# Five conditioning chunks of layer 1 accumulated during attention instead of during the output projection

## The chip, the core and the metric

The kernel runs on one core of a Trainium2 chip. The metric is the device time of one execution in microseconds; the time shown is the median of three runs. One more execution was recorded by the hardware profiler, and all rows below come from it.

Engines: TensorE (PE; its weight loads are listed as PEld), VectorE (DVE), ScalarE (ACT), GpSimd (POOL), and SyncE (SP), which only issues DMAs. Every engine works through its own queue in order.

## The reference

Two layers over 512 latent tokens of width 2048, with 256 context tokens. Layer 0 is attention: eight heads with low-rank queries and keys (A, the "long" heads here) and eight grouped-query heads (B, the "short" heads), a SiLU gate and one output projection. Layer 1 mixes by a Fourier transform. Each layer is modulated by a vector computed from `c`:

```
def modulation(cvec, ada_w, ada_b):
    m = jax.nn.silu(cvec) @ ada_w + ada_b        # 2048 -> 6144
    return jnp.split(m, 3, axis=-1)              # shift, scale, gate

def gated_out(y_a, y_b, gate, w_out):
    y = jnp.concatenate([y_a..., y_b...], axis=-1)
    return (y * jax.nn.silu(gate)) @ w_out       # the output projection, 2048 x 2048

x = post_norm(x, o_lat, g_l, ln_g[i], ln_b[i])
```

The 6144 columns of one layer's modulation are handled in twelve chunks of 512. Layer 1 needs its shift and scale (chunks 0 to 7) when its transforms begin, right behind the output projection of layer 0.

## The kernel before

All matmul operands are split in two (`split`, L41 and L44): ScalarE casts the high part, VectorE subtracts to get the low part, and `mm3` (L54) does three matmuls high x high, high x low, low x high.

**A conditioning chunk** is accumulated on VectorE, not on TensorE. `ada_steps` takes the weights of a chunk in pieces of `nk` k's: `ada_load` (L62 by way of `load`) fetches a piece of 128 x `nk` x 512 on SP, and for each k one instruction multiplies it by the column of `silu(c)` and adds it to `acc` (L195 the first, L197 the others), 16 in all. `tick` advances this generator by one piece; it is called from inside other loops, which is how the work is spread. When a chunk is complete, the next tick runs `ada_col`: four small matmuls with `ones` (L219, eight passes in the trace) turn the 512 sums into four columns in a PSUM tile, and VectorE adds the bias (L223). The loads are always pinned: `keep_in_program_order` puts an instruction behind the one traced before it on the same engine. Other instructions may be moved by the planner that orders each engine's queue when the program is built. Chunks of layer 1: 4, 0 and 5 are done before attention (in `lateral`, behind the four gate chunks of layer 0), 1, 6, 2, 7 and 3 during the output projection, 8 to 11 in the gates of layer 1.

**Attention** (`attention`) begins by splitting the six query tiles `self.cq` into `cqh` and `cql`; from then on `cq0` to `cq5` are dead, as are `sqa` and `rq`, all in the pool `keep`. Its main loop runs 64 turns, one for each head and block of 128 queries; turns 0 to 31 are the long heads, 32 to 63 the short ones. A turn does, in this order on TensorE: `fills` (projections for coming heads: `q_nope`, `q_pe` with rotary work on VectorE at L685 and L688, `k_nope`, `v_a`), `turn(i)` (six transposes of the probabilities into two PSUM tiles `pt` of the pool `psT`, which has two banks; ScalarE and VectorE empty them into `pth` and `ptl`, L778 and L779), `late` fills, `values(i - 2)` and `scores(i + 2)`, followed by the softmax on VectorE, ScalarE and GpSimd (L752 to L761). From turn 27 on the scores come ahead of `turn`. `self.pinned` is true throughout, so TensorE's order is the traced one. Two banks of `acc` serve all projections and value products.

**The output projection** (`out_proj`, called from `mixer_out`) makes four blocks of 512 columns (n). In each, 16 k's of weights are loaded two at a time, split, and multiplied with four token tiles into four PSUM banks `oacc` (there are eight); in the last block the tokens come in two groups. A block closes with the gate (`tg`, L972), the residual (L976) and statistics (L977) on VectorE. `mac_start` stands in `mixer_out` with `nk` = 2; `tick` is called after each k, from k 8 of block 0 to the end of block 2, and `mac_rest` in block 3. `ada_col` takes an `oacc` bank for its product.

Of the kernel before, what the change touches and what calls it, by code (L numbers as in the profile page):

```python
# [10 lines left out]
F32 = mybir.dt.float32  # L11
# [13 lines left out]
class Build:  # L25
# [666 lines left out]
    def attention(self, keep):  # L692
        nc, d = self.nc, self.d
        self.y_d = [self.dr.tile([128, 512], F32, name=f"y{h}") for h in range(16)]
        with ExitStack() as s:
# [17 lines left out]
            cq = []  # L713
# [152 lines left out]
            def q_b(h):  # L866
# [7 lines left out]
                def score(ps, qt):  # L874
                    o = 128 * qt
                    for a, b in segs:
                        self.mm3(ps[:, a:b], cut(qb, o, o + 128), cut(kb, a, b), True, True)
                heads[8 + h] = {"score": score, "col": 4 + 4 * h,
                                "v": lambda t: [v[:, t, 128 * j:128 * j + 128] for v in vb]}

            fills, late = {0: [(v_a, 0, 2)]}, {}
            for hp in range(4):
                b, n = 8 * hp, hp + 1
# [25 lines left out]
            scores(0)  # L909
            v_a(0, 1)  # L910
            scores(1)
            for i in range(64):
                for f, *a in fills.get(i, []):
                    f(*a)
                if 26 < i < 62:
                    scores(i + 2)
                turn(i)
                for odd in (0, 1):
                    if i in late and i % 2 == odd:
                        f, *a = late[i]  # L920
                        f(*a)
                    if i >= 2 and odd == 0:
                        values(i - 2, i % 2)
                if i < 27:
                    scores(i + 2)
            for i in (62, 63):
                values(i, i % 2)
            self.pinned = False

    def out_proj(self, w, nk, y, gate_d, res, xp, rawp, pg, tp, acp, st, kq, hold, done, every, late, first=lambda n: None):  # L930
        nc = self.nc
        for n in range(4):
            first(n)
            gt = tp.tile([128, 512], F32, name="gate", bufs=1)
            self.load(gt, gate_d[n])
            acs = [acp.tile([128, 512], F32, name="oacc") for _ in range(4)]
            groups = [(0, 1, 2, 3)] if n < 3 else [(0, 1), (2, 3)]
            for group in groups:
                end = group[-1] == 3 and n == 3
                held = []  # L940
                for q in range(nk // kq):
                    for kk in range(kq):
                        y(kq * q + kk)
                    raw = rawp.tile([128, kq, 512], F32, name="raw")
                    self.load(raw, w(n, q))
                    for kk in range(kq):
                        k = kq * q + kk
                        yh, yl = y(k)
                        hi = pg.tile([128, 512], F32R, name="pgh")
                        lo = pg.tile([128, 512], F32R, name="pgl")  # L950
                        self.split(raw[:, kk, :], hi, lo)
                        if end and k >= nk - hold:
                            held.append((k, hi, lo))
                            continue
                        for t in group:
                            o = 128 * t
                            self.mm3(acs[t], (yh[:, o:o + 128], yl[:, o:o + 128]), (hi, lo), k == 0, k == nk - 1)
                        if every and n < 3 and (n or k >= 8):
                            self.mac_hold = n == 0
                            self.tick()  # L960
                if n == 3 and not end:
                    self.mac_rest()
                if end:
                    late()
                for t in group:
                    o = 128 * t
                    for k, hi, lo in held:
                        self.mm3(acs[t], (y(k)[0][:, o:o + 128], y(k)[1][:, o:o + 128]), (hi, lo), False, k == nk - 1)
                    xr = tp.tile([128, 512], F32, name="xr")
                    self.load(xr, res(t, n))  # L970
                    g = tp.tile([128, 512], F32, name="tg")
                    ins = nc.vector.tensor_mul(out=g, in0=acs[t], in1=gt)  # L972
                    if end and t == 3:
                        self.tc.keep_in_program_order(ins)
                    xs = xp[t][:, 512 * n:512 * n + 512]
                    nc.vector.scalar_tensor_tensor(out=xs, in0=xr, scalar=ALPHA, in1=g, op0=ALU.mult, op1=ALU.add)  # L976
                    nc.vector.bn_stats(out=st[t][:, n, :], in_=xs)  # L977
                    if n == 3:
                        done(t)

    def mixer_out(self, s):
# [7 lines left out]
        with ExitStack() as c:  # L989
# [19 lines left out]
            def first(n):  # L1009
                if n == 1:  # L1010
# [4 lines left out]
                    for t, nme in zip(gb, ("lng", "lnb")):  # L1015
                        self.load(t, d[nme][0].partition_broadcast(128), True)
                    nc.scalar.activation(out=junk, in_=gb[1], func=AF.Copy, accum_out=base)

            self.mac_start(macp, lambda: tp.tile([128, 512], F32, name="mac"), lambda: acp.tile([128, 512], F32, name="oacc"),
                           [(1, 1), (1, 6), (1, 2), (1, 7), (1, 3)], 2)  # L1020

            base = rows.tile([128, 1], F32, name="base")
            junk = rows.tile([128, 2048], mybir.dt.bfloat16, name="junk")
# [81 lines left out]
            def done(t):  # L1105
# [26 lines left out]
                else:  # L1132
# [8 lines left out]
                    for cs, eng in zip(halves, (nc.gpsimd, nc.vector)):  # L1141
# [3 lines left out]
                    root(nc.gpsimd, 0, 1)  # L1145

            self.out_proj(lambda n, q: d["wo0"][n, q // 2, :, 2 * (q % 2):2 * (q % 2) + 2, :], 16, y, self.gate0, lambda t, n: d["x"][t, :, 512 * n:512 * n + 512],
                          self.xp, rawp, pg, tp, acp, st, 2, 6, done, True, late, first=first)

    def combo_tiles(self, pool):  # L1150
        def pair(shape, name):
# [550 lines left out]
```

## Time and profile before

| | us |
|---|---|
| median of three runs | 2356.12 (2350.45 to 2357.21) |
| the profiled execution | 2353.7 |
| its span, first to last instruction | 2351.9 |
| TensorE busy in the span | 2173.0 |
| VectorE busy | 1887.2 |
| ScalarE busy | 948.2 |
| GpSimd busy | 428.3 |

The busy time of TensorE is made from modelled ends of pipelined matmuls: a matmul is recorded longer than the time until the next one can start. So the distance between starts shows what TensorE could do, and the idle time in brackets shows where it stood. Of the span, attention with its preparation lies at about 608 to 968 us, the output projection at 968 to 1175.

### The profile page before, as it was taken

What the parts mean: (1) busy time and instruction counts of PE and PEld (TensorE: products, weight loads), DVE (VectorE), ACT (ScalarE), POOL (GpSimd) and SP (SyncE); (2) the same over time, 40 slices, a digit from 0 to 9 for tenths busy, and PEclk for the clock granted to TensorE, in tenths of its full rate; (3) what the DMA queues carried; (4) which work ended last, traced back from release to release, by engine and by line L of the source; (5) the groups of instructions that cost most, each with busy time, mean ns of one, the idle gap of its engine ahead of it and who ended that gap; (6) DMA issues with size and microseconds to landing.
All of it is one profiled execution on the core that took longest, in us unless ns stands there. A gap on an engine that the chain in (4) does not pass through costs nothing. (4 is left out here: it accounts for less than half of the span.)

```text
span 2351.9 us, 39267 instructions
## 1 busy us (share of the span) xinstructions
PE 2173.0 (92%) x15708; PEld 1998.8 (85%) x15708; DVE 1887.2 (80%) x2603; ACT 948.2 (40%) x1321; POOL 428.3 (18%) x407
## 2 busy tenths in 40 slices
PE   5999989989899999999978898998999998998994
PEld 3779879889888889877758898998999998998994
DVE  5456799998755569677889998779998999879898
ACT  2222344433443457422464333445344435445331
POOL 1023413100111113100252222001221224002003
PEclk9999989999999999999999999999999999999997
DMA  8852344666511122588536675535555456536332
GB/s 339 311 192 100 126 164 159 202 219 203 203 42 57 59 75 71 181 294 281 184 116 224 247 276 186 174 132 187 179 174 174 164 173 214 185 127 247 130 135 116
DMA packets 128702, 412.63 MB, mean 175 GB/s; under 512 B 14852, under 2 KB 15492, under 8 KB 126728
## 3 DMA queue, kind: packets, MB, share of 16 engines
q1 hardware_dynamic: 113144, 359.04, 44.7%
q0 software_dynamic: 8320, 31.33, 3.7%
q10 hardware_dynamic: 7056, 19.76, 2.2%
q8 instruction: 123, 2.02, 0.3%
q14 instruction: 59, 0.48, 0.1%
HBM read 347.81 MB, written 62.26 MB: 174 GB/s over the span
## 5 line engine op out<-in xcount | busy, mean ns | idle before, releaser
L54 PE MATMUL r<-bth,wl 128*128 128x256 f32 x1848 | 524.3, 284 | 16.0 <-DVE wl L44 15.7
L54 PE MATMUL r<-bth,wh 128*128 128x256 f32 x1848 | 525.6, 284 | 0.0
L54 PE MATMUL r<-btl,wh 128*128 128x256 f32 x1848 | 524.3, 284 | 1.3 <-DVE btl L44 1.0
L41 ACT CAST wh<-wraw 128x1024 fp32r<-128x1024 f32 x262 | 274.7, 1050 | 395.8 <-PE r L54 284.5
L44 DVE TENSOR_TENSOR wl<-wraw,wh 128x1024 fp32r<-128x1024 f32 x262 | 336.7, 1289 | 52.5 <-ACT wh L41 52.3
L54 PEld LDWEIGHTS r<-bth,wl 128*128 128x128 f32 x1848 | 352.1, 191 | 18.5 <-DVE wl L44 18.5
L54 PEld LDWEIGHTS r<-btl,wh 128*128 128x128 f32 x1848 | 351.1, 190 | 2.1 <-DVE btl L44 1.2
L54 PEld LDWEIGHTS r<-bth,wh 128*128 128x128 f32 x1848 | 351.5, 190 | 0.5 <-issue 0.5
L41 ACT CAST wh<-ws 128x1024 fp32r<-128x1024 f32 x183 | 191.8, 1049 | 339.9 <-PE r L54 321.4
L44 DVE TENSOR_TENSOR wl<-ws,wh 128x1024 fp32r<-128x1024 f32 x183 | 229.6, 1255 | 12.2 <-ACT wh L41 10.0
L197 DVE SCALAR_TENSOR_TENSOR mac<-macraw,cs,mac 128x512 f32<-128x512 f32 x240 | 193.6, 807 | 12.4 <-DMA macraw<-in_ada 11.0
L54 PE MATMUL r<-hlh,wl 128*128 128x256 f32 (+1 forms) x480 | 148.4, 309 | 31.8 <-DVE wl L44 31.7
L54 PE MATMUL r<-hlh,wh 128*128 128x256 f32 (+1 forms) x480 | 147.2, 307 | 0.1
L54 PE MATMUL r<-hll,wh 128*128 128x256 f32 (+1 forms) x480 | 145.8, 304 | 0.0
L54 PE MATMUL r<-bah,wl 128*128 128x256 f32 x384 | 113.3, 295 | 25.3 <-DVE wl L44 25.3
L54 PEld LDWEIGHTS r<-hlh,wl 128*128 128x128 f32 x480 | 94.7, 197 | 38.6 <-DVE wl L44 35.7
L41 ACT CAST pgh<-raw 128x512 fp32r<-128x512 f32 (+2 forms) x104 | 65.9, 660 | 124.2 <-DMA raw<-in_wo 51.4
L54 PE MATMUL r<-bah,wh 128*128 128x256 f32 x384 | 112.0, 292 | 0.0
L54 PE MATMUL r<-bal,wh 128*128 128x256 f32 x384 | 111.9, 291 | 0.0
L54 PE MATMUL oacc<-pgl,yh 128*128 128x512 f32 x256 | 103.1, 403 | 8.8 <-DVE pgl L44 8.8
L54 PE MATMUL r<-bbh,wl 128*128 128x256 f32 x384 | 108.6, 283 | 2.7 <-DVE wl L44 2.7
L54 PE MATMUL r<-bcl,wh 128*128 128x256 f32 x384 | 108.6, 283 | 1.5 <-DVE bcl L44 0.9
(489 smaller groups left out, 5707.4 us busy)
## 6 DMA issues: line engine op xcount, KB each, us to landing
macraw<-in_ada SPq DMA_DIRECT2D x72, 512.0 KB, 6.3
wraw<-in_win SPq DMA_DIRECT2D x66, 512.0 KB, 7.2
raw<-in_adas SPq DMA_DIRECT2D x64, 512.0 KB, 5.6
wraw<-in_wg SPq DMA_DIRECT2D x64, 512.0 KB, 6.9
wraw<-in_wu SPq DMA_DIRECT2D x64, 512.0 KB, 4.3
wraw<-in_wo SPq DMA_DIRECT2D x64, 512.0 KB, 4.6
macraw<-in_ada SPq DMA_DIRECT2D x112, 256.0 KB, 3.9
raw<-in_wo SPq DMA_DIRECT2D x40, 512.0 KB, 4.9
```

What stands on the lines that cost most here:

```text
L41: ins = nc.scalar.copy(out=hi, in_=src)
L44: sub = (eng or nc.vector).tensor_sub(out=lo, in0=src, in1=hi.bitcast(F32))
L54: self.pin(self.nc.tensor.matmul(ps, lhsT=a, rhs=b, start=start, stop=stop))
L197: ins = nc.vector.scalar_tensor_tensor(out=acc, in0=raw[:, k, :], scalar=col, in1=acc, op0=ALU.mult, op1=ALU.add)
```

## The change

The generator is started inside `attention`, after the first two score steps, with `nk` = 1, so that the five chunks take 80 pieces of 256 KB instead of 40 of 512 KB. A piece goes into one of the six dead query tiles in rotation (`Spare`), the sums alternate between `sqa` and half of `rq` (`spare_acc`), and the product of a finished chunk goes into a `pt` tile of the transposes' PSUM pool. Every turn calls `tick` two or three times, directly behind `turn(i)`; 80 pieces are through after turn 31, and the last product comes in turn 32. The accumulations on VectorE are not pinned there; the loads and, since `pinned` is true, the products are. `out_proj` and `mixer_out` lose the ticks, `mac_rest`, the `mac` tiles and the flag `every`.

```diff
@@ attention
+            turns = {"raw": 0, "acc": 0}
+
+            class Spare:
+                def tile(self, shape, dtype, name):
+                    turns["raw"] += 1
+                    return keep.tile([128, 512], dtype, name=name, tag=f"cq{turns['raw'] % 6}").rearrange("p (a b) -> p a b", a=1)
+
+            def spare_acc():
+                turns["acc"] += 1
+                if turns["acc"] % 2:
+                    return keep.tile([128, 512], F32, name="mac", tag="sqa")
+                return keep.tile([128, 2, 512], F32, name="mac2", tag="rq")[:, 0, :]
...
             scores(1)
+            self.mac_start(Spare(), spare_acc, lambda: pst.tile([128, 3, 128], F32, name="pt").rearrange("p a b -> p (a b)"),
+                           [(1, 1), (1, 6), (1, 2), (1, 7), (1, 3)], 1)
             for i in range(64):
...
                 turn(i)
+                for _ in range(2 + i % 2):
+                    self.tick()
                 for odd in (0, 1):
...
+            self.mac_rest()
             self.pinned = False
@@ out_proj
-                        if every and n < 3 and (n or k >= 8):
-                            self.mac_hold = n == 0
-                            self.tick()
-                if n == 3 and not end:
-                    self.mac_rest()
@@ mixer_out
-            self.mac_start(macp, lambda: tp.tile([128, 512], F32, name="mac"), lambda: acp.tile([128, 512], F32, name="oacc"),
-                           [(1, 1), (1, 6), (1, 2), (1, 7), (1, 3)], 2)
```

## Rows read from the trace of the kernel before

**Rows 1.** Windows: us, then busy us (instructions) of each engine, clock, DMA share, GB/s.

```profile
653.00:850.00 197.00, 197.00 (x1160) 162.01 (x1158) 108.01 (x209) 80.06 (x158) 31.02 (x35) 1.00 0.15 47
880.00:960.00 80.00, 80.00 (x606) 76.08 (x604) 70.01 (x164) 56.62 (x123) 30.58 (x36) 1.00 0.27 90
968.20:1174.70 206.50, 189.20 (x811) 153.32 (x809) 157.35 (x243) 61.95 (x101) 16.85 (x19) 0.96 0.74 250
```

**Rows 2.** Timeline of TensorE, output projection: start, us, instruction, [idle before <- releaser].

```profile
976.91 0.50 PE L54 MATMUL oacc<-pgh,yh 128*128 128x512 f32 x1 [2.15 <-ACT yh L41]
...
984.11 0.39 PE L54 MATMUL oacc<-pgh,yh 128*128 128x512 f32 x1
...
990.91 0.39 PE L54 MATMUL oacc<-pgh,yh 128*128 128x512 f32 x1
...
1023.84 1.86 PE L219 MATMUL oacc<-ones,mac 128*128 128x1 f32 x8 [5.57 <-DVE tg L972]
...
1026.57 0.63 PE L54 MATMUL oacc<-pgh,yl 128*128 128x512 f32 x1
1026.99 0.63 PE L54 MATMUL oacc<-pgh,yh 128*128 128x512 f32 x1
...
1082.04 0.79 PE L54 MATMUL oacc<-pgl,yh 128*128 128x512 f32 x1 [4.65 <-DVE pgl L44]
```

**Rows 3.** Waits, 967 to 1175 us: total us, times, longest us.

```profile
PE oacc L54 <- DVE pgl L44: 8.8, 5, 4.6
```

**Rows 4.** The chunk tiles, 960 to 1200 us (ns min/median/max), and its product group.

```profile
L197 DVE SCALAR_TENSOR_TENSOR mac<-macraw,cs,mac x75: 741/751/754, 983.3 to 1114.8; 128x512 f32<-128x512 f32 x75
L195 DVE TENSOR_SCALAR mac<-macraw,cs x5: 478/481/486, 982.7 to 1097.0; 128x512 f32<-128x512 f32 x5
...
L219 PE MATMUL oacc<-ones,mac 128*128 128x1 f32 x40 | 5.8, 265 | 5.7 <-DVE tg L972 5.6
```

**Rows 5.** Timeline of VectorE at the ends of column blocks 0 and 1.

```profile
1023.10 1.28 DVE L972 TENSOR_TENSOR tg<-oacc,gate 128x512 f32<-128x512 f32 x2
...
1078.79 1.34 DVE L976 SCALAR_TENSOR_TENSOR xp<-xr,tg 128x512 f32<-128x512 f32 x2 [2.08 <-DMA xr<-in_x]
...
1081.31 0.68 DVE L44 TENSOR_TENSOR pgl<-raw,pgh 128x512 fp32r<-128x512 f32 x1
```

**Rows 6.** Timeline of TensorE around the second product.

```profile
1049.58 0.95 PE L219 MATMUL oacc<-ones,mac 128*128 128x1 f32 x8
1050.39 0.49 PE L54 MATMUL oacc<-pgh,yh 128*128 128x512 f32 x1
```

**Rows 7.** Timelines of TensorE and VectorE in turns 6 and 19.

```profile
696.78 0.82 PE L775 MATMUL pt<-ident,pm 128*128 128x128 f32 x6
...
698.20 1.01 DVE L779 TENSOR_TENSOR ptl<-pt,pth 128x384 fp32r<-128x384 f32 x2
...
799.71 0.82 PE L775 MATMUL pt<-ident,pm 128*128 128x128 f32 x6
...
800.61 2.79 DVE L688 TENSOR_TENSOR ld<-acc,ra 32x512 f32<-32x512 f32 x4
803.43 1.02 DVE L779 TENSOR_TENSOR ptl<-pt,pth 128x384 fp32r<-128x384 f32 x2
```

**Rows 8.** Timelines of VectorE and TensorE in turn 5.

```profile
689.02 0.69 DVE L44 TENSOR_TENSOR kl<-acc,kh 128x512 fp32r<-128x512 f32 x1 [0.86 <-ACT kh L41]
...
689.93 0.28 PE L54 MATMUL acc<-ckv0h,pgh 128*128 128x256 f32 x1
...
693.23 0.42 DVE L44 TENSOR_TENSOR kl<-acc,kh 128x256 fp32r<-128x256 f32 x1
...
693.66 0.28 PE L54 MATMUL S<-kl,qh 128*128 128x256 f32 x1
```

**Rows 9.** Windows in the gates; the last row counts instructions on `macraw` alone.

```profile
1301.40:1443.40 142.00, 127.44 (x1036) 125.59 (x1035) 129.60 (x153) 52.09 (x54) 35.37 (x30) 0.99 0.72 256
1466.00:1586.90 120.90, 120.90 (x1010) 120.90 (x1009) 94.41 (x102) 51.39 (x56) 0.00 (x0) 1.00 0.44 153
...
1301.40:1443.40 142.00, 0.00 (x0) 0.00 (x0) 39.19 (x47) 0.00 (x0) 0.00 (x0) 0.99 0.72 256
```

**Rows 10.** The accumulation over the whole kernel (ns min/median/max, first and last start).

```profile
L197 DVE SCALAR_TENSOR_TENSOR mac<-macraw,cs,mac x240: 729/744/2901, 259.1 to 1442.3; 128x512 f32<-128x512 f32 x120
```

More of the change, by code (lines that the diff above doesn't have):

```diff
@@ L927, in attention, with out_proj @@
                 values(i, i % 2)
+            self.mac_rest()
             self.pinned = False
-    def out_proj(self, w, nk, y, gate_d, res, xp, rawp, pg, tp, acp, st, kq, hold, done, every, late, first=lambda n: None):
+    def out_proj(self, w, nk, y, gate_d, res, xp, rawp, pg, tp, acp, st, kq, hold, done, late, first=lambda n: None):
         nc = self.nc
@@ L1147, in mixer_out @@
             self.out_proj(lambda n, q: d["wo0"][n, q // 2, :, 2 * (q % 2):2 * (q % 2) + 2, :], 16, y, self.gate0, lambda t, n: d["x"][t, :, 512 * n:512 * n + 512],
-                          self.xp, rawp, pg, tp, acp, st, 2, 6, done, True, late, first=first)
+                          self.xp, rawp, pg, tp, acp, st, 2, 6, done, late, first=first)
     def combo_tiles(self, pool):
```

## Prediction

> **What bounds the kernel now.** I read the page first. In its 40 slices TensorE is busy nine tenths or more nearly everywhere, so I asked the windows view for the two stages that the change touches, attention and the first output projection. The reader should see [rows 1]: in the long-head turns (653 to 850 us) TensorE is busy for all of 197.0 us and VectorE for 108.0, 55%; in the short-head turns VectorE has 70.0 of 80; in the output projection TensorE is busy 189.2 of 206.5, at a mean clock of 0.96, with VectorE at 76% and the DMA share at 0.74, against 0.15 in attention. So attention has DMA and VectorE time to spare and no TensorE time; the projection is the reverse.
>
> Busy time hides part of the projection's slack, so next the timeline of TensorE there [rows 2]. Matmuls of 512 columns that have all they need start 0.2267 us apart (6.80 us for 30 from 984.11 to 990.91). The stage has 4 column blocks x 16 k x 4 token tiles x 3 products = 768 of them, 174.1 us. It takes 206.5 us; 32.4 are lost. Where TensorE stood: 2.15 us until 976.91, 5.57 until 1023.84, 4.65 until 1082.04. A record is 0.39 long, 0.16 more than its slot, so a stop costs its idle time plus 0.16. After the two long stops the matmuls stand 0.43 apart (1026.57 to 1026.99): the granted clock is at its lower level, 1.2 GHz, and each costs 0.2 us more. There are 10 such after the first stop, 14 after the second, 7 near the end. The waits view has five stops behind the weight split, 8.8 us [rows 3]; the longest is the one at 1082, so four stops of 4.2 us lie at the end of the stage.
>
> **What goes from the projection.** (A) The transposing products of the five chunks: 40 passes, 5.8 us of TensorE [rows 4]. (B) The stop at 1023.84 is the first of these products: it needs a ninth accumulator bank where eight are held by column blocks 0 and 1, and one comes free only when VectorE reaches the gating multiply at 1023.10 [rows 5]. Without the product nothing waits there: 5.57 + 0.16 and ten half-clock matmuls, 2.0: **7.7 us**. (C) The stop at 1082.04 waits for a weight split that VectorE does at 1081.31, behind the block's closing work, in which it also waits 2.08 us for a residual tile at 1078.79 [rows 5]. The stop is 4.65 + 0.16 + 14 x 0.2 = 7.6 us. With 75 accumulations of 0.751 and 5 of 0.481 us, 58.7 us [rows 4], gone from VectorE and 40 loads of 512 KB from the queue, splits can run ahead by up to the seven buffers of their pool, and six k's of 2.72 us cover the 10 us of closing work. I take 6.5; the ends are 0 (the closing work remains) and 7.6. (D) The stops at the start and at the end wait for stored y tiles and for normalisation work, which stay: 0, at best 3.4 us for the start, if y tiles land sooner on an emptier queue. Sum **20.0 us**, ends 13.5 and 24.5. Check: A to C in full are 21.1, D is 3.4 + 6.5, together 31.0 of the 32.4.
>
> **What comes to attention.** Nothing in TensorE's order there is idle, so each thing that makes it stand is paid in full. (E) The five products issue in 0.81 us each (1049.58 to the next start at 1050.39, [rows 6]), **4.1 us**, exact but for half a microsecond.
>
> (F) Each product now takes its accumulator from the two banks of the transposes. By the tick counts (2, 3, 2, 3 ... per turn; product c at tick 16c + 17) they fall in turns 6, 13, 19, 25 and 32, right behind that turn's transposes, and both banks are then full. TensorE's order is pinned, so it stands until ScalarE and VectorE have emptied the first, with the value products and the next scores queued behind it. In turn 6 the six transposes start at 696.78, 0.11 apart, so the product could go at 697.4; VectorE is through with the first bank at 698.20 + 0.55 = 698.75 [rows 7]: 1.4 us. In turn 19 the rotary work of the next query holds VectorE until 803.43, the transposes ended their issue at 800.4, the bank is free at 803.98: 3.6 us. Turns 13 and 25 look like 6, and I put 32 there too. Four of 1.4 and one of 3.6: **9.2 us**; ends 7.0 (the rotary work no longer first) and 18 (all as long as turn 19).
>
> (G) A stop of 2.15 us was followed by no slow matmul, one of 4.65 by fourteen [rows 2]. Turn 19 lies between: ends 0 and 2.8, I take **1.3**.
>
> (H) The 58.7 us of accumulation take VectorE from 108.0 to some 167 of 197 us, 85%. The planner may put one into any idle piece; an operation that becomes ready meanwhile waits up to 0.74 us, on average half. Where does TensorE feel it? Softmax has microseconds of slack. In turn 5 it has none [rows 8]: the key split at 689.02 ends 0.2 us ahead of the matmul at 689.93 that reuses its bank, and the one at 693.23 ends at 693.65, where the matmul that reads it starts at 693.66. Turns 5, 13 and 21 are alike: 6 places x 0.37 = 2.2. The same 0.37 in front of five bank releases is 1.9. **4.1 us**; the lower end is 0. For the upper end I take the one place where the trace has a stage with and without such work: the gates [rows 9]. Two stretches of six groups: 1010 matmuls in 120.9 us without, 1036 (24 of them products) in 142.0 with 47 accumulations; 21.1 / 47 = 0.45 us each, so 80 would cost 36. VectorE is at 91% there and the splits sit directly in front of TensorE; attention looks a turn or two ahead, so I stay near the turn's own rows.
>
> One accumulation there took 2901 ns instead of 744 [rows 10], beside GpSimd at work. The Trainium skill, GPSIMD Engine Reference, section 1 (Specifications), says that GpSimd shares its SBUF interfaces with VectorE and collides with instructions that have two SBUF inputs, which the accumulation has. By that rule attention, where GpSimd scales every probability tile, would be a bad home for it, and the slower rival below would gain; the measured 2901 agrees, the median of 744 says it is rare.
>
> (I) Loads: 80 of 256 KB in place of 40 of 512 KB, on SP, each pinned behind the SP load traced before it. A weight load of attention can stand behind one that waits for its buffer, but weights are fetched turns ahead and the DMA share is 0.15 [rows 1]: 0, and if that cover went, it would show as stops before weight matmuls, within the upper end of H. The projection's first weight tiles lie where the dead query tiles were and now come later, still well before 968: 0.
>
> Cost 4.1 + 9.2 + 1.3 + 4.1 = **18.7 us**. Net gain 20.0 - 18.7 = 1.3. The profiled execution took 2353.7 us, 2.4 under the median of the runs shown, 2356.1; 2353.7 - 1.3 = 2352.4, so **2352**.
>
> **The rivals.** *Faster*: the gain arrives whole and VectorE's idle pieces take the work without touching TensorE. C at 7.6 and part of the start, 22; cost E + F with little else, 13: net 9, **2345**; at the ends of all terms 24.5 - 11.1 = 13, 2340. For it: 45% of VectorE's time is idle in these turns. Against: the zero slack of turn 5, and five bank waits that follow from the order alone. *Slower*: VectorE becomes the bound of the long-head turns, as in the gates. Price 0.45 x 80 = 36 us at the worst instead of 4.1, so 2353.7 - 20.0 + 14.6 + 36 = 2384; at half of it **2366**. It decides from where VectorE passes some 90% in the 653 to 850 stretch; I expect 85%. *The accumulations lag* (the change does not do what it says): they end up behind the turn that wants them, and the pinned product waits for the chain. If the last five of each chunk are late, 5 x 5 x 0.744 = 19 us more: **2371**. Against it: 32 can run before the first product, since there are two accumulators.
>
> **How the numbers follow.** A measurement of this kernel can tell about 0.3%, 7 us, from no change: 2349 to 2363. Forecast, little net change: 0.56; faster rival 0.29; slower rivals 0.11 and 0.04. The forecast's own range, from half of the spread of C, F and H, is 2347 to 2360. To leave out no more than 2 in 10 I go into the faster case to 2343 and into the slower to 2364.
>
> **What would show it.** Right: the projection's 206.5 us become about 186, with no stop at its first block end and no half-clock matmuls in mid-stage; in attention five stops of over 1 us in front of products, the one in turn 19 the longest; VectorE near 85% with few waits for loads. Wrong: a stop of several us that returns at a block's end (C), products that start right behind the transposes (F), or stops before value and score matmuls all over the long-head turns (H).

## The result, and the profile after

The changed kernel is slower, by under one per cent. Its median was 2373.27 us (2367.74 to 2381.5) against 2353.52 (2348.3 to 2360.93) for the kernel before on the same chip: a ratio of 1.0086, 95% interval 1.0057 to 1.0114, some 20 us. The profiled execution took 2369.74 us (span 2368.0), 16 us more than that of before, and 3.5 under its own median; what follows explains the profiled execution.

The windows view by stage shows where. The stretches are attention (first transposes to the first matmul of the projection), the projection, the work from its end to the first matmul of the gates, and the rest. Columns: us, TensorE's busy us and instructions, granted clock, DMA share, GB/s. First the kernel before:

```profile
653.88:968.20 314.32, 313.39 (x2001) 1.00 0.21 68
968.20:1174.38 206.18, 188.88 (x809) 0.96 0.74 250
1174.38:1249.00 74.62, 58.06 (x258) 0.93 0.29 106
1249.00:2351.90 1102.90, 1023.06 (x8353) 0.97 0.53 183
```

and the kernel after:

```profile
653.19:1008.53 355.34, 335.81 (x2040) 0.96 0.35 111
1008.53:1186.26 177.73, 176.39 (x767) 0.99 0.52 170
1186.26:1266.10 79.84, 60.94 (x259) 0.89 0.30 112
1266.10:2368.00 1101.90, 1024.07 (x8353) 0.97 0.53 183
```

Attention grew by 41.0 us, at a clock of 0.96 where it had been 1.00. The projection shrank by 28.5 us and the work behind it grew by 5.2, so the gain up to the gates is 23.2. With 0.7 us less ahead of attention and 1.0 less behind the gates, 41.0 - 23.2 - 1.7 = 16.1: the difference of the spans.

**The projection** has none of the stops of [rows 2]; 768 matmuls of 0.2267 us are 174.1 of its 177.7 us. But it now ends ahead of GpSimd's part of the normalisation, and TensorE waits 7.76 us for it. The timeline of TensorE at the end of the projection, and of GpSimd ahead of that (start, us, instruction, idle before and its releaser), in the kernel after:

```profile
1186.26 0.39 PE L54 MATMUL oacc<-pgh,yl 128*128 128x512 f32 x1
1194.41 0.79 PE L54 MATMUL oacc<-dfth,macraw 128*128 128x512 f32 x1 [7.76 <-ACT macraw L1096]
...
1175.55 8.38 POOL L1152 TENSOR_TENSOR xp<-xp,lngb 128x1024 f32<-128x1024 f32 x1 [2.22 <-ACT xp L1147]
```

**Attention** lost its time in few places. Setting the first transpose of each turn beside that of the same turn before gives the excess of each turn. It is 29.3 us in the turns with a product (5.28 in turn 6, 6.41 in 13, 9.71 in 19, 3.85 in 25, 4.09 in 32 and 33), 6.0 in the turns with key splits (0.57 in turn 3, 0.93 in 5, 2.61 in 10, 1.45 in 18, 0.43 in 27), 4.1 between the last turn and the projection, and 1.6 elsewhere.

A turn with a product looks like this; TensorE in turns 6 and 19:

```profile
697.55 0.82 PE L775 MATMUL pt<-ident,pm 128*128 128x128 f32 x6
699.58 1.05 PE L219 MATMUL pt<-ones,mac 128*128 128x1 f32 x8 [1.21 <-DVE ptl L779]
...
703.29 0.63 PE L54 MATMUL S<-kl,qh 128*128 128x512 f32 x1
...
820.96 1.48 PE L219 MATMUL pt<-ones,mac 128*128 128x1 f32 x8 [3.95 <-DVE ptl L779]
```

The six transposes fill both banks, and the product waits until VectorE has read the first (1.21 us, 3.95 in turn 19). In turn 6, 2.4 us behind the product's start, the granted clock falls, and every matmul takes the time of the lower level: 0.63 for the 0.39 of [rows 2]. The windows view of the stretches behind the five products gives the granted clock, and their lengths add to 30.4 us. In turns 13 and 19 the fall comes 0.1 and 0.5 us behind the product's start, when next to nothing of the product had run:

```profile
702.00:708.60 6.60, 6.60 (x24) 0.50 0.00 0
763.40:770.20 6.80, 6.80 (x31) 0.50 0.20 63
821.40:831.60 10.20, 10.20 (x32) 0.50 0.53 169
876.00:879.40 3.40, 3.40 (x12) 0.50 0.13 23
913.60:917.00 3.40, 3.40 (x16) 0.50 0.80 222
```

The waits view of TensorE over the turns (653 to 1004 us; total us, times, longest) shows only two sorts of stop of a microsecond and more:

```profile
PE pt L219 <- DVE ptl L779: 10.0, 5, 4.0
PE acc L54 <- DVE kl L44: 4.2, 3, 2.3
```

The second sort, at its longest, is in turn 10. VectorE's timeline there:

```profile
731.96 0.75 DVE L197 SCALAR_TENSOR_TENSOR mac<-macraw,cs,mac 128x512 f32<-128x512 f32 x1 [0.84 <-DMA macraw<-in_ada]
734.09 0.75 DVE L197 SCALAR_TENSOR_TENSOR mac<-macraw,cs,mac 128x512 f32<-128x512 f32 x1 [1.38 <-DMA macraw<-in_ada]
...
735.29 1.17 DVE L197 SCALAR_TENSOR_TENSOR mac<-macraw,cs,mac 128x512 f32<-128x512 f32 x1 [0.38 <-DMA macraw<-in_ada]
736.38 0.68 DVE L44 TENSOR_TENSOR kl<-acc,kh 128x512 fp32r<-128x512 f32 x1
```

Ahead of the key split at 736.38 stand three accumulations, and VectorE stands idle for 2.6 us waiting for their loads, with the key split queued behind them. Why the loads are late is seen on SyncE's queue (timeline of its DMA issues, then its largest waits between 653 and 1008 us):

```profile
695.14 1.37 SPq L62 DMA_DIRECT2D macraw<-in_ada  x3
720.19 0.33 SPq L62 DMA_DIRECT2D raw<-in_wqn  x1
720.56 1.12 SPq L62 DMA_DIRECT2D macraw<-in_ada  x2
...
SPq L62 <- DVE pgl L44: 115.9, 14, 23.6
SPq L62 <- DVE yt L795: 107.1, 13, 31.8
```

A weight load waits at the head of the queue for its buffer, 23.6 us between 696.5 and 720.2, and the accumulation loads behind it come in bursts. The queue waited like this in the kernel before as well, but no accumulation's load stood behind it; its waits for weight buffers there, from 653 to 968 us:

```profile
SPq L62 <- DVE pgl L44: 103.3, 10, 20.4
```

The 4.1 us behind the last turn are one stop, with ScalarE waiting for a stored y tile:

```profile
1008.53 0.50 PE L54 MATMUL oacc<-pgh,yh 128*128 128x512 f32 x1 [3.94 <-ACT yh L41]
...
1007.86 1.14 ACT L41 CAST yh<-yf 128x512 fp32r<-128x512 f32 x2 [5.93 <-DMA y<-yt]
```

### The profile page after: what moved, and what is told of

Same layout as the page of the kernel before. It is cut to its first block, busy times and chain, and to the rows that moved or that the text cites. A ratio compares the mean times of both kernels' runs of the same rounds, so it can differ in the third digit from the quotient of the medians.

```text
span 2368.0 us, 39336 instructions
## 1 busy us (share of the span) xinstructions
PE 2190.0 (92%) x15708; PEld 2012.8 (85%) x15708; DVE 1888.1 (80%) x2603; ACT 949.3 (40%) x1321; POOL 434.9 (18%) x407
## 5 line engine op out<-in xcount | busy, mean ns | idle before, releaser
L54 PE MATMUL r<-bth,wl 128*128 128x256 f32 x1848 | 525.0, 284 | 16.3 <-DVE wl L44 16.1
L44 DVE TENSOR_TENSOR pgl<-raw,pgh 128x512 fp32r<-128x512 f32 (+2 forms) x104 | 74.9, 738 | 61.6 <-ACT pgh L41 61.4
L757 ACT ACTIVATE pm<-S,nb,qs 128x768 f32<-128x768 f32 x64 | 63.6, 994 | 125.6 <-DVE nb L754 125.5
```

Of the source, the lines that this page charges most:

```text
L44: sub = (eng or nc.vector).tensor_sub(out=lo, in0=src, in1=hi.bitcast(F32))
L54: self.pin(self.nc.tensor.matmul(ps, lhsT=a, rhs=b, start=start, stop=stop))
L757: nc.scalar.activation(out=pm, in_=ps[:, :768], func=AF.Exp, scale=self.qs[:, col:col + 1], bias=nb, accum_out=sm)
```

## The experiments

Ratios are against the kernel before, timed beside it on the same chip, with 95% intervals. "Attention" and "projection" are stretches as above (before: 314.3 and 206.2 us, after: 355.3 and 177.7), and they come from one profiled execution of each kernel.

**One half of the change: nothing in the projection, nothing in attention.** The kernel before without the five chunks (their columns hold a constant; their accumulator tiles are kept so that addresses stay):

```diff
-            self.mac_start(macp, ..., [(1, 1), (1, 6), (1, 2), (1, 7), (1, 3)], 2)
-                        if every and n < 3 and (n or k >= 8):
-                            self.mac_hold = n == 0
-                            self.tick()
```

> The kernel before with the five chunks left out altogether (constants in those columns), its projection's tile layout kept. It shows what the projection gains when the work leaves. If the stops at the block ends were due to it, as predicted, the projection falls from 206 to about 178 us and, after some 4 us given back at its end, the kernel to about 2329. If those stops return in another form (closing work of a block), the projection stays above 190 and the time above 2340.

Measured: 2335.08 us, 0.9919 (0.9893 to 0.9945). Attention 314.2, projection 184.6; up to the gates 259.7 us against 280.8. One stop of 5.3 us behind a weight split is left, 10 us ahead of the projection's end, where the changed kernel has its 7.76 us behind it. So even a free home for the chunks is worth some 19 us by the ratio and 21 up to the gates, and attention must take the work for less than that.

**The other half without its products.** The changed kernel with the accumulations and loads in attention but no products (their columns hold a constant):

```diff
-                (self.ada_col if layer else self.ada_row)(layer, chunk, acc, row)
+                if not self.skip:
+                    (self.ada_col if layer else self.ada_row)(layer, chunk, acc, row)
```

> Leaves out the five products and their VectorE adds (those columns of shift and scale hold a constant); loads and accumulations are as in the changed kernel. What is left over the kernel without any of this work is the price of the accumulations and loads alone. Theory 1: attention is about 8 us longer than before (the four stops at key splits, 5.6 us, and some 2 us in the short-head turns), the time about 2344. Rival (VectorE load): attention stays some 35 us longer, 2368.

Measured: 2348.15 us, 0.9988 (0.9972 to 1.0005). Attention 329.4 at a clock of 1.00, no stretch at the lower level in the turns. So of the 41 us, 15 come with accumulations and loads (4.1 of them at the start of the projection, see e6) and 26 with the products.

**Products ahead of the turn's transposes.**

```diff
+                for _ in range(2 + i % 2):
+                    self.tick()
                 turn(i)
-                for _ in range(2 + i % 2):
-                    self.tick()
```

> The two or three ticks of a turn are called ahead of its transposes instead of behind them, so each product finds a free bank of the transposes' pool; all else is as in the changed kernel. Theory 1 (the stop in front of each product, and the half clock that follows it, are what the change costs): the five product turns lose their 10 us of stops and some 14 us of half-clock matmuls, the long-head turns take about 16 us more than before instead of 37, and the time falls by 24 us from the changed kernel's 2373, to about 2349. Rival (the accumulations load VectorE, and TensorE waits for it everywhere): nothing of that changes, the time stays within 5 us of 2373. Half way (the stop goes but a product of one-column passes still brings the clock down): about 2361.

Measured: 2357.44 us, 1.0024 (1.0009 to 1.0038). Attention 338.3. The stops in front of products for VectorE's bank reads are gone; the transposes behind the product wait for its bank in one place worth counting (3.27 us in turn 19), and one product waits 0.93 us for its accumulation. The clock fell behind these two only, 3.4 us each. With the order turned round the products' price over e3 is 8.8 us in place of 25.9: the bank wait and what follows it were the larger part of it.

**Products behind the last turn**, with five accumulators of their own and four load buffers:

```diff
+                if self.later is not None:
+                    self.later.append((layer, chunk, acc, row))
...
             self.mac_rest()
+            for a in self.later:
+                self.ada_col(*a)
```

> The accumulations stay where the change puts them, but the five sums lie in five tiles of their own (loads rotate over four query tiles instead of six) and the five products follow the last value product of attention. Theory 1: no stops and no half clock in the turns, and the five products fill the 4 us in which TensorE waits for the first y tiles anyway: about 29 us under the changed kernel, 2344. Rival (VectorE load): within 5 us of 2373, or more with only four load buffers.

Measured: 2354.97 us, 1.0006 (0.999 to 1.0022). Attention 333.3, of which the stretch behind the last turn holds 9.8 more than before; the turns are near those without products (9.2 us over before, 11.0 in e3). The 2344 that I expected was missed, since the products did not fit into the wait for y. And the clock fell among them: their 40 one-column passes run from 971.32 to 977.88 us, TensorE had not stood for longer than 0.55 us ahead of them, and 2.2 us into them the granted clock goes to the lower level, for 13.6 us (windows: us, busy, clock, ...):

```profile
965.00:973.40 8.40, 7.85 (x68) 1.00 0.09 33
973.50:987.10 13.60, 10.32 (x36) 0.50 0.77 258
```

**Steps behind the value products.** The same ticks, some 2 us later in TensorE's order:

```diff
                 turn(i)
-                for _ in range(2 + i % 2):
-                    self.tick()
...
                         values(i - 2, i % 2)
+                for _ in range(2 + i % 2):
+                    self.tick()
```

> The changed kernel with the accumulation steps, and with them the five products, moved behind the turn's second half of value products, about 2 us later on TensorE, when VectorE has emptied the bank that the product takes. Theory (stops lead to the low clock): the stops of 10.0 us ahead of the products go, with them the five low-clock stretches (30.6 us at half clock, some 14 us of time), and attention falls from 355 to about 332 to 336 us; the time falls by some 20 us to about 2351 to 2355. Rival (the one-column product itself counts as rest): the stops go but the low-clock stretches behind all five stay; attention falls by 10 us only, to about 345 us, and the time to about 2363. Second rival: the product takes a bank from the transposes that follow, which stop in its stead; then stops of 1 to 4 us stand before transposes or score products, and the time is between.

Measured: 2362.33 us, 1.0033 (1.0018 to 1.0049). Attention 338.7. The profiled execution was the fastest of ten (2353.9 us), 8.4 under their median, so the others may hold more falls than it shows. It separates the stop from the product: three products now start without a stop (turns 6, 13, 25), two keep one (turns 19 and 32). TensorE's timeline at the first and the fourth, and the windows (us, busy, clock, ...) behind all five in order:

```profile
697.00 1.05 PE L219 MATMUL pt<-ones,mac 128*128 128x1 f32 x8
697.91 0.47 PE L54 MATMUL S<-kpeh,stk 128*128 128x512 f32 x1
...
807.53 1.05 PE L219 MATMUL pt<-ones,mac 128*128 128x1 f32 x8 [2.44 <-DVE ptl L779]
...
698.00:704.00 6.00, 6.00 (x42) 1.00 0.02 6
757.00:763.00 6.00, 6.00 (x44) 1.00 0.95 320
808.70:815.50 6.80, 6.80 (x17) 0.50 0.27 77
859.00:865.00 6.00, 6.00 (x30) 1.00 0.65 171
894.00:897.40 3.40, 3.40 (x15) 0.50 0.25 64
```

The clock fell behind the two with a stop and stayed at 1.00 behind the three without. Those three turns are 1.29, 1.21 and 1.29 us longer than before: the price of a product that nothing disturbs.

**A wider product.** Each product against 128 columns of ones in place of one:

```diff
-            self.pin(nc.tensor.matmul(ps[:, i:i + 1], lhsT=..., rhs=self.ones[:, 0:1], ...))
+            self.pin(nc.tensor.matmul(ps[:, w * i:w * i + w], lhsT=..., rhs=self.ones[:, 0:w], ...))
```

> The changed kernel with each of the five products taken against 128 equal columns of ones instead of one (the same result 128 times; one column of it is used). Nothing else moves, so the stops of about 10 us ahead of the products stay. Theory (the stop and what else is short around it set the clock): all five low-clock stretches stay, 30 us in all, and the time stays at 2373 or rises by the wider products' own 2 to 4 us, to 2373 to 2377. Rival (the one-column product itself is seen as rest): with 128 columns the low-clock stretches shrink or go, attention falls by 8 to 14 us and the time to about 2360 to 2367.

Measured: 2365.22 us, 1.0052 (1.0034 to 1.0071). Attention 347.9. The stops in front of the products are as before the edit: 1.21, 1.82, 4.18, 1.21 and 1.35 us. The windows behind them:

```profile
698.40:705.20 6.80, 6.80 (x47) 1.00 0.02 7
761.50:764.90 3.40, 3.40 (x17) 0.50 0.00 2
816.10:822.90 6.80, 5.53 (x20) 0.50 0.43 143
869.00:875.80 6.80, 6.80 (x38) 1.00 0.46 141
904.00:907.40 3.40, 3.35 (x26) 1.00 0.38 100
```

Two of five fell, for 10.2 us, where the one-column products had all five and 30.4. (A further 6.8 us at the lower level came behind a key split's stop of 1.94 us in turn 10.) Five places in one execution decide little: e11, below, has one-column products with stops nearly as long, three falls and 13.6 us. All traces together say more. Counting a fall that began inside a stop or up to 3 us behind it, the clock fell at 20 of the 22 stops of 0.9 to 2.4 us ahead of a one-column product, at 6 of 32 such stops ahead of other matmuls, and at 1 of the 4 ahead of a 128-column product; at the 16 stops of over 3 us in the turns it fell, or was down already, whatever stood behind. Nine single products with no stop on either side (e1, e7, e14, e15) had no fall. So both theories held a part: a single product needs a stop next to it, and a short stop mostly brings a fall only where one-column passes stand behind it. Five products together need no stop, as e2 shows.

**No loads in attention.** One row is loaded, all accumulations read it:

```diff
+        if self.one is not None:
+            if self.one == 0:
+                self.one = raw
+                self.load(raw, src[chunk, q, :, o], True)
+            return self.one, None
```

> The changed kernel without the loads of the conditioning weights' rows in attention: one row is loaded, and all 80 accumulations read it, so the five chunks' values are wrong and VectorE's and TensorE's work is the same. Theory (the loads): accumulations come late and in bunches since their loads stand on SyncE's queue behind weight loads that wait for their buffers, up to 24 us, and what bunches up in front of a key split delays it; without loads the stops at the key splits of turns 3, 10, 18 and 27 fall from 6.0 us to under 2 us in all, attention falls by 4 to 6 us, and the time to about 2366 to 2369. Rival (VectorE's own time, 0.74 us an accumulation): the stops stay at 5 to 6 us and the time at 2371 to 2374.

Measured: 2358.21 us, 1.0018 (1.0008 to 1.0029). Attention 340.5. The waits view of TensorE over the turns:

```profile
PE pt L224 <- DVE ptl L784: 8.6, 5, 3.5
...
PE acc L54 <- DVE kl L44: 0.2, 1, 0.2
```

The key splits are on time in every turn: the excess of turns 3, 5, 10, 18 and 27 is 0 in place of 6.0, with the same accumulations on VectorE. It is the loads, not VectorE's time. The turns with products are 9.5 us shorter as well; the clock fell behind three products only (13.6 us), though the stops were nearly as long. So a stop of 1.2 to 1.5 us doesn't bring the clock down each time. Attention is 14.8 us shorter in all; whether the loads bear on the clock, or three falls in place of five were chance, one trace doesn't tell (after, e6 and e9, with loads, have five of five).

**Loads issued further ahead.**

```diff
-        nxt = self.ada_load(*items[0])
+        many = 4 if self.pinned else 1
+        ready = [self.ada_load(*it) for it in items[:many]]
```

> The changed kernel with the rows of the conditioning weights loaded four steps ahead instead of one (six buffers, as before). Theory (load waits): the stops of TensorE at the key splits of turns 3, 10, 18 and 27 (0.6, 2.6, 1.5 and 0.4 us lost there) come from VectorE standing at an accumulation whose load has not landed, 1 to 2.4 us in front of the key split; with the loads ahead they fall to 1.5 us or less in all, and so do the waits for the weight rows in the waits of VectorE (19 us in all) to under 3 us; the time falls by 4 to 7 us, to about 2366 to 2369. Rival (VectorE's own time): the accumulations' 0.74 us each, two or three a turn, are what makes the key split late; then the stops stay within 1 us of 5 in sum, and the time stays at 2373.

Measured: 2424.32 us, 1.0308 (1.0286 to 1.033). The edit also took hold in an earlier stage, which became 53 us longer, so the time says nothing here; attention does: 356.0, with 6.2 us at and just behind the key splits, and VectorE waiting for these loads 13 times, 9.4 us in all, as against 12 times and 7.8 us after. Four steps ahead in the program is not earlier on the chip when the queue stands: the loads leave in the same bursts.

**Loads issued by GpSimd.**

```diff
-        self.load(raw, src[...], True)
+        if self.by_pool:
+            self.tc.keep_in_program_order(self.nc.gpsimd.dma_start(out=raw, in_=src[chunk, q, :, o]))
```

> The changed kernel with the loads of the weights' rows issued by GpSimd, where no weight load stands ahead of them, instead of SyncE. Theory (SyncE's queue holds the loads): they are issued within a turn or two of their tick, the waits of VectorE for them (9 to 19 us in after) fall under 3 us, the stops at the key splits fall from 6.0 us to 1 to 3 us, and the time by 3 to 5 us, to about 2367 to 2370. Rival (GpSimd): GpSimd scales the scores of each turn and waits for VectorE 214 us in the turns; the issues delay that by their own time, the transposes that wait for it come late, and attention rises by 5 to 20 us, the time to 2378 to 2393. Second rival (VectorE's own time): no change, 2373.

Measured: 2394.09 us, 1.0165 (1.0148 to 1.0181). Attention 374.1. VectorE's waits in the turns, and TensorE in turn 25:

```profile
DVE mac L201 <- DMA macraw<-in_ada: 36.0, 30, 2.6
...
877.27 1.84 PE L223 MATMUL pt<-ones,mac 128*128 128x1 f32 x8 [6.36 <-DVE mac L201]
```

The size is that of the GpSimd rival (attention 18.7 us longer), the way is mostly another. Transposes wait for GpSimd's scaling for 2.9 us only. But GpSimd, in order behind its own waits for VectorE, issues the loads later still (36.0 us of waits in place of 7.8), the accumulations fall behind, and two products wait for their last accumulation, 13.1 us in all. This is the "accumulations lag" of the prediction's rivals, and slower than that rival's 2371.

**Old addresses in the projection.**

```diff
+            for _ in range(2):
+                nc.gpsimd.memset(tp.tile([128, 512], F32, name="mac"), 0.0)
```

> The changed kernel with one thing added: two unused tiles of 2 KB each are taken in the projection's pool, where the accumulators used to lie, so that every later tile of the projection has the address that it has in the kernel before. Theory (addresses): the stop of 3.9 us ahead of the projection's third block, which waits for ScalarE's splitting of y, which waits for a load of y, is there since the tiles of y now lie over attention's output tiles and must wait for their last store; with the old addresses the start falls back to the two stops of 0.65 and 1.58 us of the kernel before, and the time falls by 3 to 4 us, to about 2366 to 2369. Rival (lateness): the stop is there since attention ends behind its own VectorE work; then it stays at 3.9 us and the time stays at 2373. The attention's turns keep their 5 low-clock stretches in both.

Measured: 2369.76 us, 1.0075 (1.0059 to 1.009). The stop of 3.94 us is gone (attention 351.3; two stops of 0.65 and 0.62 us in its place). It came from the addresses: without the accumulators' tiles in the projection's pool the tiles behind them move, and the first tiles of y wait for attention's last stores. But the projection is 2.7 us longer in return, and the intervals of the two ratios overlap: a cause found, worth little.

**Both together, at the end**: five accumulators, products behind the last turn, old addresses.

> e2 and the two unused tiles of e6 together: each of the five chunks accumulates in space of its own, the five products stand behind the last turn, and the projection's tiles have their old addresses. If the two causes add up (e2 took 2354.97 us with a start stop of 3.3 us in it; e6 took the attention from 355.3 to 351.3 us), attention takes some 329 to 330 us and the time is about 2350 to 2352, level with or just under the kernel before. Rival: the five products behind the last turn fill the time in which the projection's first tiles come in, so the start stop was hidden behind them in e2 and its removal brings nothing; then attention stays at 333 us and the time at 2355.

Measured: 2351.63 us, 0.9986 (0.9975 to 0.9996). The fastest version that computes everything, under both kernels, but only 0.14% under the one before. Attention 332.2: the rival was right on one point, TensorE still waits 3.57 us for the first y tile, now behind the five products. This stop has a cause of its own. From 961.7 to 980.5 us SyncE stands at a weight load of the projection until a product has run (it seems that the load goes to where an accumulator lies), and the loads of y stand behind it. Its queue's largest wait from 960 to 985 us:

```profile
SPq L62 <- PE pt L222: 18.8, 1, 18.8
```

In e2 the same wait is 19.2 us. The clock falls among the products here too, 2.8 us into them, for 10.2 us. With GpSimd's loads on top:

> e10 with the loads issued by GpSimd as in e12. If the loads' place on SyncE's queue makes the key splits late, this is the best of them all: attention some 324 to 326 us and a time of about 2345 to 2348, under both kernels. If it is VectorE's own time, it equals e10 (2350 to 2352). If GpSimd's issues delay its scaling, it is over e10 by 5 to 20 us.

Measured: 2382.77 us, 1.0118 (1.0104 to 1.0133). Attention 360.3: the delay of the loads again, at the key and query splits.

**Quiet turns.** e7 with the old addresses and no step in turns ahead of a key split or with the rotation of queries; four steps in the others, then three:

```diff
-                for _ in range(2 + i % 2):
+                for _ in range(0 if i in (3, 4, 8, 9, 11, 12, 16, 17, 19, 20, 24, 25) else 4):
```

> e7 (steps behind the value products) with the two unused tiles of e6, and no accumulation step in the turns that come before a key split or that hold the rotation of queries (3, 4, 8, 9, 11, 12, 16, 17, 19, 20, 24, 25), four in each of the others: two products fall into turns 7 and 14, one into turn 22, the last two into turns 28 and 32. Theory (what a product costs is set by what VectorE does in its turn: in e7 the two products with a stop ahead of them, 2.4 us in turn 19 behind the rotation and 1.4 us in turn 32, were followed by the low clock, and the three without were not): the three products up to turn 22 have no stop above 0.7 us and no low clock behind them, attention falls from e7's 338.7 us to 326 to 330 us (4.1 of it by the two tiles), and the time to about 2348 to 2352. Rival (any one-column product inside the turns lowers the clock now and then, and loads that come late delay the key splits whatever the turn of the step): attention stays at 333 to 336 us and the time at 2355 to 2359.

> e14 with three steps in each turn that has them instead of four: the accumulations reach to turn 38, products fall into turns 7, 18, 28, 33 and behind 38, three of them into the turns that attend to the second half of heads, where TensorE waits for nothing and VectorE has the least time to spare. If the loads come late because four steps ask for them in one turn, key splits are on time here and attention is 1 to 3 us shorter than e14's in the turns up to 27. If VectorE's free time decides, each product behind turn 27 costs a stop of 1 to 1.5 us and a low-clock stretch, attention is 3 to 6 us longer than e14's and the time 2352 to 2356.

Measured: 2364.74 us, 1.0049 (1.0033 to 1.0065), and 2369.73, 1.0063 (1.0049 to 1.0076). My theory fell. Attention is 347.7 and 351.6, longer than e7's 338.7 (the fastest execution of e7 and, in the second, the slowest of six; the intervals of e7 and the first overlap). Four steps in one turn load VectorE in just the turns that hold the product; TensorE in turns 22 and 32 of the first, and VectorE in turn 22:

```profile
838.73 1.05 PE L219 MATMUL pt<-ones,mac 128*128 128x1 f32 x8 [1.85 <-DVE ptl L779]
...
906.00 1.84 PE L219 MATMUL pt<-ones,mac 128*128 128x1 f32 x8 [5.21 <-DVE mac L197]
...
836.86 0.75 DVE L197 SCALAR_TENSOR_TENSOR mac<-macraw,cs,mac 128x512 f32<-128x512 f32 x1 [1.10 <-DMA macraw<-in_ada]
```

In turn 32 VectorE is busy for 10.3 of the 11.0 us up to 907; in turn 22 it stands idle until a load lands, with the read of the bank queued behind. Four of the five products have a stop (1.69, 0.94, 1.85, 5.21 us), each with 3.4 or 6.8 us at the lower clock; the fifth has none, and no fall. In the second, key splits waited up to 3.54 us (turn 18), and the two late products 4.75 and 5.49 us for their accumulation.

## Why the prediction was wrong

The forecast was 2352 (2343 to 2364); the time is 2373. The gain side held: 23.2 us up to the gates against 20.0. Attention cost 41.0 against 18.7. The mechanism of the stops was right, that of their price was not. Term by term, the measured sizes from the excess of the turns:

| term | predicted | measured | from |
|---|---|---|---|
| A to D, projection up to the gates | -20.0 | -23.2 | 28.5 in the projection, 5.2 given back behind it |
| E, products | 4.1 | 6.3 | 5 x 1.26, e7's turns without a stop |
| F, waits for banks | 9.2 | 10.0 | five stops, waits view |
| G, lower clock | 1.3 | 13.0 | what is left: 29.3 - 6.3 - 10.0 |
| H, VectorE's interference | 4.1 | 1.6 | turns without product or key split |
| I, loads: key splits | 0 | 6.0 | gone in e11 |
| in no term: start of the projection | 0 | 4.1 | gone in e6 |

Two rows are not clean. G is what is left over in the turns with products, and these lose 2.7 us in e3 without any product. And e11 prices the loads at 14.8 us: the 6.0 of I, and 9.5 in the product turns that the table books under F and G; what is left for G there is 4.9.

**G is the step that failed**, by 11.7 us. I took [rows 2] to say that a stop of 2.15 us brings no slow matmul and one of 4.65 does, and so counted turn 19 alone. The row of 2.15 us is a stop with a full stream of 512-column matmuls behind it; here one-column products and a bank wait stand side by side, and the clock fell behind stops of 1.21 us. In all traces the clock fell at 20 of 22 stops of 0.9 to 2.4 us ahead of such products, at 6 of 32 ahead of other matmuls. [rows 2] gave no warning of that. Its stop of 5.57 us stands in front of a product too, but there the clock had fallen inside the stop, half a microsecond ahead of the product at 1023.84:

```profile
1018.00:1023.30 5.30, 0.28 (x2) 1.00 0.88 324
1023.34:1030.10 6.76, 6.26 (x19) 0.50 0.84 256
```

The Trainium skill, TensorE: Matmul & The Clock Gate, section "A second HAM failure mode: psum-queue depth-cycling", tells of a kernel that cycles through PSUM banks, whose TensorE stands briefly and often between groups of matmuls, with the clock falling and rising again; five bank waits of 1.2 to 4.0 us with 30.4 us at half clock agree with it in kind.

**I was the second**: 6.0 us at the key splits where I wrote 0, and 14.8 in all by e11. My reason, that weights are fetched turns ahead and the DMA share is 0.15, is true and beside the point. Because weights are asked for turns ahead, their loads stand at the head of SyncE's queue waiting for a buffer, and anything behind them waits too. I had named that wait and priced it by what it does to weights, not to the accumulations behind them. e11 shows the loads as the cause; that SyncE's standing queue is what makes them late rests on the queue's own rows and on e9 and e12, where loads asked for earlier, or from a busier engine, were no better or worse. In e10 and e2 the queue's wait and what stands behind it, the loads of y, can be read directly. A queue free of held loads wasn't tried. The 4.1 us at the start of the projection are a side effect that the diff doesn't show: removing two tiles from a pool moves its neighbours.

**H** had the right place, the key splits without slack [rows 8], and the wrong cause. VectorE was busy 135.5 of the 197 us of [rows 1]'s first stretch, 69%, where I expected 85: 57 of the 80 accumulations stand in that stretch, and 13 had run ahead of it. And without loads the key splits lose nothing. The slower rival, VectorE as the bound, is refuted: it gave 2366, near the time, for a reason that isn't there. The clash with GpSimd cost little: the accumulations of the turns have a median of 751 ns and a longest of 1358. (The 2901 ns of [rows 10] lie at 355.8 us, ahead of attention, beside a GpSimd instruction of 2987 ns; in the gates, where I had put them, the longest is 1325.)

**F was right** to a microsecond, in size and order: five stops, turn 19 the longest with 3.95 (3.6 forecast), turns 6 and 25 with 1.21. **E** was short by 0.4 us a product: I took the product's own issue from [rows 6], and the matmuls behind it start slower as well (0.47 long for 0.39, and some 0.4 apart instead of 0.23, in e7's turn 6).

**C was right, D half**: the projection's mid-stage stops went, and its end stops too, which I had left in place. What waited at the end, the normalisation, did stay: it became the 7.76 us stop behind the projection. Part by part the gain is 28.5 - 5.2 = 23.2.

What stays open: why the time from the gates to the end differs from profile to profile, 1101.9 us after, 1110.7 in e3, 1109.1 in e5, 1102.9 before. It takes back up to 8 us of what a run gained. The lower-clock stretches there lie differently from profile to profile; no run here separates them from the rest.

## What to carry to other kernels

Work moved into a stage that has no idle TensorE time can cost far more than its own duration: here bank waits next to one-column products brought a lower clock, and its 13 us were more than the waits (10) or the products (6). Put such products where their bank is already empty, or ahead of whatever fills it, and not all together: five in a row brought the clock down by themselves. Before adding a load to a queue, look at what the queue itself waits for: one that fetches far ahead is a queue that stands, and a small urgent load behind it comes late, with all that the waiting engine has queued. Price the removal by itself first (here 19 us); it bounds what any new home may cost.

## What the runs showed of the hardware

- A fall of the clock behind a stop of 1.21 us with one-column products around it: 6.6 us at 0.50, at 702.0. In the same kernel the stop of 2.35 us in front of a value product in turn 10 had no fall behind it.
- The same product with 128 columns: stops of 1.21, 1.21 and 1.35 us with the clock staying at 1.00.
- Five one-column products together, 40 passes, with no stop of over 0.55 us in the 9 us ahead: the clock at 0.50 from 2.2 us into them in e2 and, in e10, from 2.8 us, for 13.6 and 10.2 us (with the stop for y, 3.3 and 3.6 us, behind them).
- The same GpSimd multiply of 128x1024 took 8.4 us in seven kernels (after, e1, e3, e6, e7, e10, e11), 6.55 before and 2.5 in the eight others. It was slow where the projection ran without a long stop near its end (177 to 180 us) and fast where it had one of 5.0 to 6.6 us (183 to 186 us), so that all of these reach the gates in about the same time, 257 to 262 us from the projection's start. Which of the two leads to the other isn't shown.
